# Triangular inverses of two head pairs' chunks: four 64x64 diagonal blocks at a time instead of two 128x128 matrices twice

## The chip, the cores and the metric

The kernel runs on one core of a Trainium2 chip. The metric is the device time of one execution in microseconds; the median of 3 runs is 3688.35 us (3687.65 to 3692.61). PE is TensorE (its matmuls; PEld its weight loads), DVE is VectorE, ACT is ScalarE, POOL is GpSimd.

## The reference

Two model blocks run one after the other on 256 tokens of width 2048 in float32. The change touches two branches of the second block: RWKV-7 (16 heads of 64, in 8 pairs) and the gated delta rule (GDN, 8 heads of 128, in 4 pairs). Both are recurrences over time that the kernel computes in two chunks of 128 tokens. Of the GDN branch the reference says:

```
    lower = jnp.einsum('nbhcd,nbhsd->nbhcs', k_beta, k) * decay_strict
    eye = jnp.eye(GDN_CHUNK, dtype=q.dtype)
    t_mat = lax.linalg.triangular_solve(eye + lower, jnp.broadcast_to(eye, lower.shape),
                                        left_side=True, lower=True)
    u = jnp.einsum('nbhcs,nbhse->nbhce', t_mat, v * beta[..., None])
    w = jnp.einsum('nbhcs,nbhsd->nbhcd', t_mat, k_beta * jnp.exp(g_cum)[..., None])
```

RWKV's step is written in the reference as a scan over single tokens (state times decay, plus two outer products). In chunks it needs the same thing: the inverse of the identity plus a strictly lower triangular 128x128 matrix per head and chunk.

## The kernel before

Weights stream from memory in tiles of 128x1024. ScalarE rounds each to a high part (`whi`, line 276), VectorE forms the rest (`wlo`, line 280), and PE multiplies three times per tile (lines 287 to 289, `mm3`): these are the dense products, with 128x128 weights and 256 or 512 moving columns. They are made by generators in a queue; `fill` runs the next one up to its next tile (24 or 12 products).

The RWKV pairs (`rwkv_pair`) and then the GDN pairs (`gdn_pair`) are generators as well. `weave` keeps up to two pairs going, steps each in turn and, by a credit of 0.44 (RWKV) or 0.6 (GDN) per step, calls `fill` between steps. So a pair's small products stand on PE between runs of dense ones. All engines work off their queues in order; the order is fixed when the program is made, by the order of the code and by a scheduler that may pull ready work ahead.

A pair has two heads and two chunks, so four matrices L to invert. `inverse2` takes two of them (128x128, side by side in a tile of 256 columns) and starts from Y, the inverse of the 2x2 diagonal blocks (lines 1727 to 1733: mask with M1, transpose, subtract from the identity). Five times it doubles the blocks, b = 2, 4, 8, 16, 32: with L masked to the block half it forms Z by a product (line 1738), transposes Y (line 1740), ScalarE takes both out of PSUM (line 1742), a second product (line 1747) gives the correction, and VectorE subtracts it (line 1748). Products are full 128x128 though Y is zero outside its diagonal blocks of up to 64. The closing step fills in the 64x64 block between the two diagonal blocks of 64 (lines 1751 to 1765) with 64x64 products (lines 1754 and 1763) and transposes (line 1759). `both` steps the two calls of `inverse2` of a pair in turn, and a `yield` stands behind each half of a step, where other work may be put. There are 24 calls.

The inverse is used as weights of one 128x128 product per head and chunk: line 1964 in RWKV (64 moving columns), lines 2155, 2156 and 2169 in GDN, where line 2156 has the inverse as the moving side.

Of the kernel before, what the change touches and what calls it, by code (L numbers as in the profile page):

```python
# [11 lines left out]
AF = mybir.ActivationFunctionType  # L12
ALU = mybir.AluOpType
# [69 lines left out]
def layout(i):  # L83
    a = {}
# [31 lines left out]
    p = Pack()  # L116
# [5 lines left out]
    p = Pack()  # L122
# [14 lines left out]
    r = np.arange(128)  # L137
# [19 lines left out]
    G, R, SU = 0, 4112, 8400  # L157
# [18 lines left out]
    for n, nm in enumerate(("s5_c_re_2", "s5_c_im_2")):  # L176
        c = i[nm][0].reshape(32, 2, 16, 64).transpose(1, 3, 0, 2)
# [3 lines left out]
    p = Pack()  # L181
# [17 lines left out]
    p = Pack()  # L199
    lo_ = (r[:, None] > r[None]).astype(np.float32)  # L200
    up = (r[:, None] <= r[None]).astype(np.float32)
    p.add("mask4", np.concatenate([lo_, lo_.T, up, up], 1))
    p.add("M1", (r[:, None] // 2 == r[None] // 2) & (r[:, None] % 2 == 1) & (r[None] % 2 == 0))
    for b in (2, 4, 8, 16, 32):
        p.add(f"M{b}", (r[:, None] // (2 * b) == r[None] // (2 * b)) & (r[:, None] % (2 * b) >= b) & (r[None] % (2 * b) < b))
    e1 = np.zeros((128, 31), np.float32)
    e1[:, 15] = 1
    p.add("E1", e1)
# [24 lines left out]
class K:  # L233
# [1474 lines left out]
        return [x for j in range(8) for x in (self.cm(A["glu"], j, (yh, yl), evg, nk=8), self.cm(A["w2sz"], j, hT, evz, ("sz", j)))]  # L1708


    def inverse2(self, L, res):

        nc = self.nc
        V, PL, mm = nc.vector, nc.gpsimd, nc.tensor.matmul
        cb = lambda n: self.cp(n, "cb")[:, None, :].to_broadcast([128, 2, 128])
        id2 = self.ident[:, None, :].to_broadcast([128, 2, 128])
        v2 = lambda x: x.rearrange("p (a b) -> p a b", a=2)
        T = [slice(128 * i, 128 * i + 128) for i in range(2)]
        U = [slice(256 + 128 * i, 384 + 128 * i) for i in range(2)]

        def masked(b):
            lb = self.r1()
            PL.tensor_tensor(v2(lb), v2(L), cb(f"M{b}"), op=ALU.mult)  # L1723
            return lb


        lm, lb = masked(1), masked(2)
        yield
        ps = self.bank()
        for i in range(2):  # L1730
            nc.tensor.transpose(ps[:, T[i]], lm[:, T[i]], self.ident)
        Y = self.r1()
        V.tensor_tensor(v2(Y), id2, v2(ps[:, 0:256]), op=ALU.subtract)
        yield
        for b in (2, 4, 8, 16, 32):
            ps = self.bank()
            for i in range(2):
                mm(ps[:, T[i]], lb[:, T[i]], Y[:, T[i]], start=True, stop=True)  # L1738
            for i in range(2):
                nc.tensor.transpose(ps[:, U[i]], Y[:, T[i]], self.ident)  # L1740
            zx = self.r2()
            nc.scalar.activation(zx, ps, AF.Copy)
            if b < 32:
                lb = masked(2 * b)
            yield
            for i in range(2):
                mm(ps[:, U[i]], zx[:, U[i]], zx[:, T[i]], start=True, stop=True)  # L1747
            V.tensor_tensor(Y, Y, ps[:, 256:512], op=ALU.subtract)
            yield

        h, l = slice(0, 64), slice(64, 128)
        ps = self.bank()
        for i in range(2):
            mm(ps[h, 64 * i : 64 * i + 64], L[l, 128 * i : 128 * i + 64], Y[l, 128 * i + 64 : 128 * i + 128], start=True, stop=True)  # L1754
        zx = self.r1()
        nc.scalar.activation(zx[h, 0:128], ps[h, 0:128], AF.Copy)
        ps = self.bank()
        for i in range(2):
            nc.tensor.transpose(ps[h, 64 * i : 64 * i + 64], Y[h, 128 * i : 128 * i + 64], self.ident[h, h])
        V.tensor_copy(zx[h, 128:256], ps[h, 0:128])  # L1760
        yield
        for i in range(2):
            mm(ps[h, 128 + 64 * i : 192 + 64 * i], zx[h, 128 + 64 * i : 192 + 64 * i], zx[h, 64 * i : 64 * i + 64], start=True, stop=True)  # L1763
        y = v2(Y)[h, :, 64:128]
        V.tensor_tensor(y, y, ps[h, 128:256].rearrange("p (a b) -> p a b", a=2), op=ALU.subtract)
        yield
        res.append(Y)

    def both(self, a, b):

        for _ in a:
            next(b, None)
            yield
        for _ in b:
            yield


    def rwkv_front(self, pl, hT, kT):
# [86 lines left out]
    def rwkv_pair(self, j, keep, out):  # L1865
        nc, A = self.nc, self.A
        V, ACT, PL, mm = nc.vector, nc.scalar, nc.gpsimd, nc.tensor.matmul
# [12 lines left out]
        lw, a = self.r1(), self.r1()  # L1880
# [47 lines left out]
        ACT.activation(tm, pt, AF.Copy)  # L1928
        yield
        m4 = self.cp("mask4", "cb")  # L1930
        mats, Ls, invs, res = {}, [], [], []
        Ps = [slice(0, 64), slice(64, 128)]
        tks = [slice(0, 128), slice(128, 256)]
        for q in range(2):

            tk = tks[q]
            Ls.append(self.r1())
            pms = [self.bank() for _ in Ps]
            for n, (x, y) in enumerate(((al, be), (ka, al), (be, rh), (ka, rh))):
                for pm, P in zip(pms, Ps):  # L1940
                    mm(pm[:, n * 128 : n * 128 + 128], x[P, tk], y[P, tk], start=True, stop=True)
            for h, pm in enumerate(pms):
                V.tensor_tensor(Ls[q][:, h * 128 : h * 128 + 128], pm[:, 0:128], m4[:, 0:128], op=ALU.mult)  # L1943
                mats[h, q] = self.r2()
                V.tensor_tensor(mats[h, q][:, 0:384], pm[:, 128:512], m4[:, 128:512], op=ALU.mult)
                yield
            res.append([])
            invs.append(self.inverse2(Ls[q], res[q]))
        yield from self.both(*invs)
        py = self.bank()  # L1950
        S1 = None
        for q in range(2):
            U, tk = res[q][0], tks[q]
            v = [tm[:, q * 128 + P.start : q * 128 + P.stop] for P in Ps]
            pa = self.bank()
            if q:
                mm(pa[:, 0:128], al[:, tk], S1, start=True, stop=False)
            for h in range(2):
                mm(pa[:, h * 64 : h * 64 + 64], mats[h, q][:, 0:128], v[h], start=q == 0, stop=q == 0 or h == 1)
            sa = self.r1()  # L1960
            ACT.activation(sa[:, 0:128], pa[:, 0:128], AF.Copy, scale=-1.0)
            yield
            for h in range(2):
                mm(pa[:, 128 + h * 64 : 192 + h * 64], U[:, h * 128 : h * 128 + 128], sa[:, h * 64 : h * 64 + 64], start=True, stop=True)
            V.tensor_copy(sa[:, 128:256], pa[:, 128:256])
# [12 lines left out]
            yield  # L1978
# [3 lines left out]
        sl = [slice(n * 64, n * 64 + 64) for n in range(4)]  # L1982
# [5 lines left out]
        r = self.rstd(self.br, st[:, 2], 4, 64.0, 64e-5)  # L1988
# [7 lines left out]
        f = self.r1()  # L1996
# [99 lines left out]
    def gdn_pair(self, h0, out, T, qk, pss, keep, beta, hb, g, gc, be, kd, gw, rs):  # L2096
        nc, A = self.nc, self.A
        V, ACT, PL, mm = nc.vector, nc.scalar, nc.gpsimd, nc.tensor.matmul
        m4 = self.cp("mask4", "cb")
        low, tri = m4[:, 0:128], m4[:, 256:384]  # L2100
        sets = [(q, d, h0 + d) for q in range(2) for d in range(2)]
        sl = [slice(128 * i, 128 * i + 128) for i in range(4)]
        v4 = lambda x: x.rearrange("p (a b) -> p a b", a=4)
        tk = sl[0:2]
# [8 lines left out]
        E1, E2 = self.r2(), self.r2()  # L2113
        for n, (q, d, h) in enumerate(sets):
            c = gc[:, q, h : h + 1]
# [17 lines left out]
            V.scalar_tensor_tensor(E2[:, sl[n]], pk[:, sl[n]], beta[:, q, h : h + 1], E2[:, sl[n]], op0=ALU.mult, op1=ALU.mult)  # L2133
        V.tensor_tensor(E1, E1, pq, op=ALU.mult)
        yield
        res = [[], []]
        inv = self.both(self.inverse2(E2[:, 0:256], res[0]), self.inverse2(E2[:, 256:512], res[1]))
        next(inv)
        yield

# [8 lines left out]
            next(inv)  # L2149
            yield  # L2150
        yield from inv
        U0, U1 = res[0][0], res[1][0]
        pa, po = self.bank(), self.bank()
        for d in range(2):
            mm(pa[:, sl[d]], U0[:, sl[d]], vt[:, sl[d]], start=True, stop=True)
            mm(pa[:, sl[2 + d]], kt[:, sl[2 + d]], U1[:, sl[d]], start=True, stop=True)
        vn, w, st = self.r2(), self.r1(), self.r1()
        V.tensor_copy(vn[:, 0:256], pa[:, 0:256])
        ACT.activation(w, pa[:, 256:512], AF.Copy, scale=-1.0)
# [6 lines left out]
            mm(po[:, sl[d]], E1[:, sl[d]], vn[:, sl[d]], start=True, stop=True)  # L2166
        yield
        for d in range(2):
            mm(pa[:, sl[2 + d]], U1[:, sl[d]], vt[:, sl[2 + d]], start=True, stop=False)  # L2169
            mm(pa[:, sl[2 + d]], w[:, sl[d]], st[:, sl[d]], start=False, stop=True)  # L2170
        V.tensor_copy(vn[:, 256:512], pa[:, 256:512])
        yield
# [73 lines left out]
```

## Time and profile before

| | us |
|---|---|
| median of 3 runs | 3688.35 |
| profiled execution | 3693.79 |
| its span | 3692.0 |
| PE busy | 3506.5 (95%) |
| VectorE busy | 2494.6 (68%) |
| ScalarE busy | 1626.7 (44%) |
| GpSimd busy | 404.1 (11%) |

RWKV pairs run from 2639 to 3232 us of the span, GDN pairs from 3232 to 3552 us. In the timeline each row is a group of like instructions one behind the other on an engine: when the first started, how long from there to the end of the last, and how many. Matmuls are pipelined, so a row's length counts the way through the array of its last one as well, and rows overlap; the distance between starts is the better measure of what a matmul takes from PE.

### The profile page before, as it was taken

The page shows a single profiled execution, that of the slowest core. Times are in us where ns is not written, and L with a number is a line of the kernel's source. Part 1 is how long each engine was busy: PE and PEld are TensorE (multiplying, and loading weights), DVE is VectorE, ACT ScalarE, POOL GpSimd, SP SyncE. Part 2 cuts the span into 40 slices and gives each one's busy share as a digit, 9 for nine tenths or more (in the row PEclk, how much of TensorE's full clock was granted, in tenths as well). Part 3 has the DMA queues.
Part 4 walks back from the last instruction along what each step waited for, and adds up shares of the span by engine and source line. Part 5 has one row for each costly group of instructions (what it writes and reads, how often), then busy time and mean ns, then how long its engine had stood idle before and what let it go on. Part 6 is the DMA issues. An engine that isn't in the chain of part 4 may idle for free. (4 is left out here: it accounts for less than half of the span.)

```text
span 3692.0 us, 59371 instructions
## 1 busy us (share of the span) xinstructions
PE 3506.5 (95%) x22760; PEld 3124.3 (85%) x22760; DVE 2494.6 (68%) x4329; ACT 1626.7 (44%) x2768; POOL 404.1 (11%) x487
## 2 busy tenths in 40 slices
PE   4799998999999899999999998999999999999998
PEld 4788766999999899988878887786899889888987
DVE  6767787788788654566555557988765556665665
ACT  2245543444444344444545555333444444444444
POOL 0000020000000000000000002333322222021210
PEclk9899998999999999999999999999999999999999
DMA  8875777777544855566666665655533433344455
GB/s 299 279 243 185 230 252 244 256 237 248 175 156 159 266 194 183 183 199 201 211 240 210 209 208 193 200 166 179 169 117 110 144 127 115 115 137 156 147 173 188
DMA packets 237080, 710.83 MB, mean 193 GB/s; under 512 B 33835, under 2 KB 61564, under 8 KB 235516
## 3 DMA queue, kind: packets, MB, share of 16 engines
q1 hardware_dynamic: 196044, 661.59, 54.4%
q10 hardware_dynamic: 40752, 45.44, 3.8%
q8 instruction: 179, 2.93, 0.3%
q14 instruction: 105, 0.86, 0.1%
HBM read 673.86 MB, written 32.55 MB: 191 GB/s over the span
## 5 line engine op out<-in xcount | busy, mean ns | idle before, releaser
L276 ACT ACTIVATE whi<-raw 128x1024 fp32r<-128x1024 f32 (+2 forms) x1006 | 1053.4, 1048 | 1583.5 <-PE acc L288 623.9
L280 DVE TENSOR_TENSOR wlo<-raw,whi 128x1024 fp32r<-128x1024 f32 (+2 forms) x1006 | 1260.6, 1255 | 668.7 <-ACT whi L276 666.9
L287 PE MATMUL acc<-hh,whi 128*128 128x256 f32 x3936 | 1145.3, 291 | 19.1 <-ACT whi L276 16.4
L289 PE MATMUL acc<-hh,wlo 128*128 128x256 f32 x3936 | 1132.0, 288 | 24.4 <-DVE wlo L280 24.0
L288 PE MATMUL acc<-hl,whi 128*128 128x256 f32 x3936 | 1126.5, 286 | 1.0 <-DVE hl L280 1.0
L289 PEld LDWEIGHTS acc<-hh,wlo 128*128 128x128 f32 x3936 | 764.5, 194 | 38.6 <-DVE wlo L280 31.1
L287 PEld LDWEIGHTS acc<-hh,whi 128*128 128x128 f32 x3936 | 765.9, 195 | 32.2 <-ACT whi L276 18.8
L288 PEld LDWEIGHTS acc<-hl,whi 128*128 128x128 f32 x3936 | 764.9, 194 | 2.9 <-DVE hl L280 1.6
L288 PE MATMUL acc<-wlo,wh 128*128 128x512 f32 x1024 | 402.1, 393 | 4.5 <-DVE wlo L280 3.9
L287 PE MATMUL acc<-whi,wh 128*128 128x512 f32 x1024 | 396.2, 391 | 4.8 <-ACT whi L276 3.2
L289 PE MATMUL acc<-whi,wl 128*128 128x512 f32 x1024 | 400.4, 391 | 0.0
L288 PE MATMUL acc<-wlo,hh 128*128 128x512 f32 (+1 forms) x672 | 267.2, 398 | 12.1 <-DVE wlo L280 12.0
L287 PE MATMUL acc<-whi,hh 128*128 128x512 f32 (+1 forms) x672 | 270.8, 406 | 4.6 <-ACT whi L276 3.2
L289 PE MATMUL acc<-whi,hl 128*128 128x512 f32 (+1 forms) x672 | 264.4, 394 | 0.0
L288 PEld LDWEIGHTS acc<-wlo,wh 128*128 128x128 f32 x1024 | 193.5, 189 | 50.9 <-DVE wlo L280 10.5
L287 PEld LDWEIGHTS acc<-whi,wh 128*128 128x128 f32 x1024 | 192.7, 188 | 46.2 <-ACT whi L276 4.5
L289 PEld LDWEIGHTS acc<-whi,wl 128*128 128x128 f32 x1024 | 193.4, 189 | 39.9
L339 DVE SCALAR_TENSOR_TENSOR ada<-raw,u,ada 128x1024 f32<-128x1024 f32 x150 | 194.3, 1295 | 32.9 <-DMA raw<-in_ada_dram 32.0
L288 PEld LDWEIGHTS acc<-wlo,hh 128*128 128x128 f32 x672 | 128.8, 192 | 41.9 <-DVE wlo L280 17.2
L287 PEld LDWEIGHTS acc<-whi,hh 128*128 128x128 f32 x672 | 128.3, 192 | 41.6 <-issue 8.6
L289 PEld LDWEIGHTS acc<-whi,hl 128*128 128x128 f32 x672 | 128.8, 192 | 26.3 <-DVE hl L402 0.2
L1723 POOL TENSOR_TENSOR r<-r,cb 128x256 f32<-128x256 f32 x144 | 132.3, 941 | 155.9 <-DVE r L1943 38.1
(580 smaller groups left out, 4254.0 us busy)
## 6 DMA issues: line engine op xcount, KB each, us to landing
raw<-in_pu_dram SPq DMA_DIRECT2D x256, 512.0 KB, 3.4
raw<-in_pv_dram SPq DMA_DIRECT2D x252, 512.0 KB, 3.5
raw<-in_ada_dram SPq DMA_DIRECT2D x192, 512.0 KB, 4.6
raw<-in_w2gate_dram SPq DMA_DIRECT2D x96, 512.0 KB, 3.4
raw<-in_wo_dram SPq DMA_DIRECT2D x64, 512.0 KB, 4.3
raw<-in_w2br_dram SPq DMA_DIRECT2D x48, 512.0 KB, 3.4
raw<-in_w2g_dram SPq DMA_DIRECT2D x48, 512.0 KB, 3.4
raw<-in_w1e_dram SPq DMA_DIRECT2D x32, 512.0 KB, 4.7
```

The costliest lines, as they stand in the source:

```text
L276: nc.scalar.activation(hi, src, AF.Copy)
L280: self.lo = e.tensor_sub(lo, src, hi.bitcast(F32)).ins
L287: mm(out, shi, mhi, start=start, stop=False)
L288: mm(out, shi, mlo, start=False, stop=False)
L289: mm(out, slo, mhi, start=False, stop=stop)
L339: nc.vector.scalar_tensor_tensor(acc, w, c, acc, op0=ALU.mult, op1=ALU.add)
L1723: PL.tensor_tensor(v2(lb), v2(L), cb(f"M{b}"), op=ALU.mult)
```

## The change

`inverse4` replaces two calls of `inverse2` under `both`. All four matrices of a pair are taken at once, and of each only the two diagonal blocks of 64: GpSimd copies the upper left block of each matrix (partitions 0 to 63) beside the lower right one (partitions 64 to 127), so that one tile of 256 columns holds all eight blocks, four on either half of the partitions. Each product is 64x64; the list `each` goes through the four matrices and for each first through the upper half (rows and columns 0 to 63 of the array), then the lower half (rows and columns 64 to 127). The transposes of the inner steps become products with a 64x64 identity. The masks become 64 columns wide, with a new constant I64. The closing step forms the off-diagonal block and writes it, with the opposite sign, into a second tile R (upper half), beside a copy of the lower diagonal block (lower half). `by_inverse` then applies the inverse in two products: one 64x64 for the first 64 rows of the result, and one with all 128 rows and 64 columns of weights for the other 64. Line 2156 becomes two products in the same manner. The names in the rows below are PE's output and inputs: `sm` is a PSUM bank, `r` a tile of the pair, `cs` the identity, `u` a tile of line 1878's small product, `acc`, `hh`, `hl`, `whi`, `wlo` and `B` belong to the dense products.

The first place is on PE, in the fourth doubling step of the first RWKV pair. Before:

```order
L289 MATMUL acc_25930<-hh_21989,wlo_4412_25934 128x256
L1738 MATMUL sm_25973<-r_4366_25668,r_4404_25892 128x128 x2
L1740 MATMUL sm_25973<-cs_63,r_4366_25668 128x128 x2
L1738 MATMUL sm_25982<-r_4368_25673,r_4407_25901 128x128 x2
L1740 MATMUL sm_25982<-cs_63,r_4368_25673 128x128 x2
L1878 MATMUL sm_25991<-u_3690_22102,r_4423_25992 128x256
```

Now:

```order
L290 MATMUL acc_25942<-hh_21989,wlo_4398_25946 128x256
L1745 MATMUL sm_25988<-r_4363_25670,r_4393_25913 64x64 x8
L1747 MATMUL sm_25988<-cs_63,r_4363_25670 64x64 x8
L1882 MATMUL sm_26009<-u_3690_22102,r_4406_26010 128x256
L1883 MATMUL sm_26009<-u_3690_22102,r_4406_26010 128x256
```

Eight full-size operations in two banks have become sixteen of 64x64 in one bank, at the same place between dense products.

The second place is on PE, the closing step of the same pair. Before:

```order
L289 MATMUL acc_26130<-hh_21989,wlo_26134 128x256
L1754 MATMUL sm_26180<-r_4366_25668,r_4328_25490 64x64 x2
L1759 MATMUL sm_26185<-cs_63,r_4366_25668 64x64 x2
L1754 MATMUL sm_26189<-r_4368_25673,r_4342_25561 64x64 x2
L1759 MATMUL sm_26194<-cs_63,r_4368_25673 64x64 x2
```

Now:

```order
L290 MATMUL acc_26156<-hh_21989,wlo_26160 128x256
L1762 MATMUL sm_26211<-r_4363_25670,r_4328_25490 64x64
L1763 MATMUL sm_26212<-cs_63,r_4363_25670 64x64
L1762 MATMUL sm_26211<-r_4363_25670,r_4328_25490 64x64
L1763 MATMUL sm_26212<-cs_63,r_4363_25670 64x64
```

Product and transpose now alternate one by one (four times; two of the four are shown), not two by two.

The third place is on PE, the first use of the inverse in the same pair. Before:

```order
L1941 MATMUL sm_26283<-r_4451_26107,r_4450_26106 128x128
L1941 MATMUL sm_26284<-r_4451_26107,r_4450_26106 128x128
L1964 MATMUL sm_26259<-r_4481_26262,r_4366_25668 128x64 x2
L287 MATMUL acc_26248<-B_3683_22089,whi_26278 128x256
L288 MATMUL acc_26248<-B_3684_22090,whi_26278 128x256
```

Now:

```order
L1944 MATMUL sm_26308<-r_4432_26133,r_4431_26132 128x128
L1778 MATMUL sm_26284<-r_4460_26287,r_4363_25670 64x64
L1779 MATMUL sm_26284<-r_4460_26287,r_4444_26209 64x64
L1778 MATMUL sm_26284<-r_4460_26287,r_4363_25670 64x64
L1779 MATMUL sm_26284<-r_4460_26287,r_4444_26209 64x64
L288 MATMUL acc_26273<-B_3683_22089,whi_26303 128x256
```

Each of the two products has become two, of different shapes of weights in turn (the sizes in a row are those of the output).

The core of the diff:

```diff
-    for b in (2, 4, 8, 16, 32):
-        p.add(f"M{b}", (r[:, None] // (2 * b) == r[None] // (2 * b)) & (r[:, None] % (2 * b) >= b) & (r[None] % (2 * b) < b))
+    x, y = r[:, None] % 64, np.arange(64)[None]
+    for b in (1, 2, 4, 8, 16, 32):
+        p.add(f"M{b}", (x // (2 * b) == y // (2 * b)) & (x % (2 * b) >= b) & (y % (2 * b) < b))
+    p.add("I64", x == y)
...
-    def inverse2(self, L, res):
+    def inverse4(self, L, res):
...
+        h, l = slice(0, 64), slice(64, 128)
+        PL.tensor_copy(v4(L)[h, :, 64:128], v4(L)[h, :, 0:64])
+        Ld = v4(L)[:, :, 64:128]
+        C = [slice(64 * n, 64 * n + 64) for n in range(4)]
+        G = [slice(256 + 64 * n, 320 + 64 * n) for n in range(4)]
+        each = [(C[n], G[n], P) for n in range(4) for P in (h, l)]
...
         lm, lb = masked(1), masked(2)
         yield
         ps = self.bank()
-        for i in range(2):
-            nc.tensor.transpose(ps[:, T[i]], lm[:, T[i]], self.ident)
+        for c, _, P in each:
+            mm(ps[P, c], lm[P, c], self.ident[P, P], start=True, stop=True)
...
         for b in (2, 4, 8, 16, 32):
             ps = self.bank()
-            for i in range(2):
-                mm(ps[:, T[i]], lb[:, T[i]], Y[:, T[i]], start=True, stop=True)
-            for i in range(2):
-                nc.tensor.transpose(ps[:, U[i]], Y[:, T[i]], self.ident)
+            for c, _, P in each:
+                mm(ps[P, c], lb[P, c], Y[P, c], start=True, stop=True)
+            for c, g, P in each:
+                mm(ps[P, g], Y[P, c], self.ident[P, P], start=True, stop=True)
             zx = self.r2()
-            nc.scalar.activation(zx, ps, AF.Copy)
+            ACT.activation(zx, ps, AF.Copy)
             if b < 32:
                 lb = masked(2 * b)
             yield
-            for i in range(2):
-                mm(ps[:, U[i]], zx[:, U[i]], zx[:, T[i]], start=True, stop=True)
+            for c, g, P in each:
+                mm(ps[P, g], zx[P, g], zx[P, c], start=True, stop=True)
             V.tensor_tensor(Y, Y, ps[:, 256:512], op=ALU.subtract)
             yield
...
+        R = self.r1()
+        PL.tensor_copy(R[l], Y[l])
+        ps, px = self.bank(), self.bank()
+        for n in range(4):
+            mm(ps[h, C[n]], L[l, 128 * n : 128 * n + 64], Y[l, C[n]], start=True, stop=True)
+            nc.tensor.transpose(px[h, C[n]], Y[h, C[n]], self.ident[h, h])
+        zx = self.r2()
+        ACT.activation(zx[h, 0:256], ps[h, 0:256], AF.Copy)
+        V.tensor_copy(zx[h, 256:512], px[h, 0:256])
         yield
...
+        for n in range(4):
+            mm(px[h, G[n]], zx[h, G[n]], zx[h, C[n]], start=True, stop=True)
+        V.tensor_scalar(R[h], px[h, 256:512], -1.0, None, op0=ALU.mult)
         yield
+        res += [Y, R]
+
+    def by_inverse(self, out, U, n, x, stop=True):
+        mm = self.nc.tensor.matmul
+        c = slice(64 * n, 64 * n + 64)
+        mm(out[0:64], U[0][0:64, c], x[0:64], start=True, stop=stop)
+        mm(out[64:128], U[1][:, c], x, start=True, stop=stop)
...
             for h in range(2):
-                mm(pa[:, 128 + h * 64 : 192 + h * 64], U[:, h * 128 : h * 128 + 128], sa[:, h * 64 : h * 64 + 64], start=True, stop=True)
+                self.by_inverse(pa[:, 128 + h * 64 : 192 + h * 64], U, 2 * q + h, sa[:, h * 64 : h * 64 + 64])
...
         for d in range(2):
-            mm(pa[:, sl[d]], U0[:, sl[d]], vt[:, sl[d]], start=True, stop=True)
-            mm(pa[:, sl[2 + d]], kt[:, sl[2 + d]], U1[:, sl[d]], start=True, stop=True)
+            self.by_inverse(pa[:, sl[d]], U, d, vt[:, sl[d]])
+            c, o = slice(128 + 64 * d, 192 + 64 * d), 256 + 128 * d
+            mm(pa[:, o : o + 64], kt[0:64, sl[2 + d]], U[0][0:64, c], start=True, stop=True)
+            mm(pa[:, o + 64 : o + 128], kt[:, sl[2 + d]], U[1][:, c], start=True, stop=True)
...
         for d in range(2):
-            mm(pa[:, sl[2 + d]], U1[:, sl[d]], vt[:, sl[2 + d]], start=True, stop=False)
+            self.by_inverse(pa[:, sl[2 + d]], U, 2 + d, vt[:, sl[2 + d]], stop=False)
```

## Rows read from the trace of the kernel before

**Rows 1.** The page: span, busy time of each engine, granted clock in slices.
```profile
span 3692.0 us, 59371 instructions
...
PE 3506.5 (95%) x22760; PEld 3124.3 (85%) x22760; DVE 2494.6 (68%) x4329; ACT 1626.7 (44%) x2768; POOL 404.1 (11%) x487
...
PEclk9899998999999999999999999999999999999999
```
**Rows 2.** Windows, RWKV and GDN pairs: busy us (instructions), granted clock, DMA.
```profile
core 0: us, PE busy (x) PEld busy (x) DVE busy (x) ACT busy (x) POOL busy (x), PEclk, DMA share, GB/s
2639.00:3232.00 593.00, 580.08 (x4534) 536.37 (x4534) 364.01 (x653) 260.05 (x546) 149.46 (x214) 0.99 0.38 123
3232.00:3552.00 320.00, 314.62 (x2017) 275.21 (x2016) 184.23 (x295) 141.02 (x263) 78.37 (x87) 0.99 0.44 142
```
**Rows 3.** Groups by line: count, busy us, mean ns of one, idle before.
```profile
L1723 POOL TENSOR_TENSOR r<-r,cb 128x256 f32<-128x256 f32 x144 | 132.3, 941 | 155.9 <-DVE r L1943 38.1 <-DVE r L2056 32.4 <-PE sm L1941 15.0
L1738 PE MATMUL sm<-r,r 128*128 128x128 f32 x480 | 74.5, 278 | 0.9 <-DVE r L1748 0.7
L1742 ACT ACTIVATE r<-sm 128x512 f32<-128x512 f32 x120 | 66.8, 594 | 16.2 <-PE sm L1740 15.2
...
L1748 DVE TENSOR_TENSOR r<-r,sm 128x256 f32<-128x256 f32 x120 | 49.7, 419 | 76.4 <-PE sm L1747 52.3 <-issue 8.1 <-ACT whi L276 6.4
L1740 PE MATMUL sm<-cs,r 128*128 128x128 f32 x240 | 45.8, 273 | 0.0
```
**Rows 4.** Timeline, PE, a full-size burst: start us, us to the last end.
```profile
2666.98 0.28 PE L289 MATMUL acc<-hh,wlo 128*128 128x256 f32 x1
2667.10 1.05 PE L1747 MATMUL sm<-r 128*128 128x128 f32 x8
...
2668.11 0.28 PE L288 MATMUL acc<-hl,whi 128*128 128x256 f32 x1
```
**Rows 5.** Timeline, PE, a use of the inverse.
```profile
2842.80 0.55 PE L1964 MATMUL sm<-r,r 128*128 128x64 f32 x4
```
**Rows 6.** Timeline, PE, a 64x64 burst on one corner.
```profile
2772.86 0.28 PE L289 MATMUL acc<-hh,wlo 128*128 128x256 f32 x1
2773.07 0.67 PE L1763 MATMUL sm<-r 64*64 64x64 f32 x8
2773.68 0.39 PE L287 MATMUL acc<-hh,whi 128*128 128x256 f32 x1
2773.90 0.28 PE L288 MATMUL acc<-hl,whi 128*128 128x256 f32 x1
```
**Rows 7.** Timeline, PE, the closing step's products and transposes.
```profile
2767.31 0.28 PE L289 MATMUL acc<-hh,wlo 128*128 128x256 f32 x1
2767.52 0.44 PE L1754 MATMUL sm<-r,r 64*64 64x64 f32 x4
2767.89 0.30 PE L1759 MATMUL sm<-cs,r 64*64 64x64 f32 x2
2768.12 0.44 PE L1754 MATMUL sm<-r,r 64*64 64x64 f32 x4
2768.50 0.30 PE L1759 MATMUL sm<-cs,r 64*64 64x64 f32 x2
2768.72 0.39 PE L287 MATMUL acc<-hh,whi 128*128 128x256 f32 x1
2768.95 0.28 PE L288 MATMUL acc<-hl,whi 128*128 128x256 f32 x1
```
**Rows 8.** Timeline, PE, 64-row products on upper and lower rows.
```profile
2652.33 0.28 PE L289 MATMUL acc<-hh,wlo 128*128 128x256 f32 x1
2652.54 1.16 PE L1941 MATMUL sm<-r,r 64*128 64x128 f32 x16
...
2653.85 0.28 PE L288 MATMUL acc<-hl,whi 128*128 128x256 f32 x1
```
**Rows 9.** Timeline, PE, products on four column strips.
```profile
2363.19 1.07 PE L1637 MATMUL sm<-r,r 128*32 128x256 f32 x16
```

More of the change, by code (lines that the diff above doesn't have):

```diff
@@ L202, in layout @@
     p.add("mask4", np.concatenate([lo_, lo_.T, up, up], 1))
-    p.add("M1", (r[:, None] // 2 == r[None] // 2) & (r[:, None] % 2 == 1) & (r[None] % 2 == 0))
-    for b in (2, 4, 8, 16, 32):
-        p.add(f"M{b}", (r[:, None] // (2 * b) == r[None] // (2 * b)) & (r[:, None] % (2 * b) >= b) & (r[None] % (2 * b) < b))
+    x, y = r[:, None] % 64, np.arange(64)[None]
+    for b in (1, 2, 4, 8, 16, 32):
+        p.add(f"M{b}", (x // (2 * b) == y // (2 * b)) & (x % (2 * b) >= b) & (y % (2 * b) < b))
+    p.add("I64", x == y)
     e1 = np.zeros((128, 31), np.float32)
@@ L1708, in s5_back @@
         return [x for j in range(8) for x in (self.cm(A["glu"], j, (yh, yl), evg, nk=8), self.cm(A["w2sz"], j, hT, evz, ("sz", j)))]
-    def inverse2(self, L, res):
+    def inverse4(self, L, res):
         nc = self.nc
[L1714 to L1719, printed above, removed]
+        V, ACT, PL, mm = nc.vector, nc.scalar, nc.gpsimd, nc.tensor.matmul
+        v4 = lambda x: x.rearrange("p (a b) -> p a b", a=4)
+        cb = lambda n: self.cp(n, "cb")[:, None, :].to_broadcast([128, 4, 64])
+        h, l = slice(0, 64), slice(64, 128)
[4 more added lines that the diff above has]
+        each = [(C[n], G[n], P) for n in range(4) for P in (h, l)]
         def masked(b):
             lb = self.r1()
-            PL.tensor_tensor(v2(lb), v2(L), cb(f"M{b}"), op=ALU.mult)
+            PL.tensor_tensor(v4(lb), Ld, cb(f"M{b}"), op=ALU.mult)
             return lb
@@ L1729, in inverse2 @@
         ps = self.bank()
-        for i in range(2):
-            nc.tensor.transpose(ps[:, T[i]], lm[:, T[i]], self.ident)
+        for c, _, P in each:
+            mm(ps[P, c], lm[P, c], self.ident[P, P], start=True, stop=True)
         Y = self.r1()
-        V.tensor_tensor(v2(Y), id2, v2(ps[:, 0:256]), op=ALU.subtract)
+        V.tensor_tensor(v4(Y), cb("I64"), v4(ps[:, 0:256]), op=ALU.subtract)
         yield
@@ L1745, in inverse2 @@
             yield
-            for i in range(2):
-                mm(ps[:, U[i]], zx[:, U[i]], zx[:, T[i]], start=True, stop=True)
+            for c, g, P in each:
+                mm(ps[P, g], zx[P, g], zx[P, c], start=True, stop=True)
             V.tensor_tensor(Y, Y, ps[:, 256:512], op=ALU.subtract)
             yield
[L1751 to L1760, printed above, removed]
+        R = self.r1()
[7 more added lines that the diff above has]
+        V.tensor_copy(zx[h, 256:512], px[h, 0:256])
         yield
[L1762 to L1765, printed above, removed]
+        for n in range(4):
+            mm(px[h, G[n]], zx[h, G[n]], zx[h, C[n]], start=True, stop=True)
+        V.tensor_scalar(R[h], px[h, 256:512], -1.0, None, op0=ALU.mult)
         yield
[L1767 to L1775, printed above, removed]
+        res += [Y, R]
[4 more added lines that the diff above has]
+        mm(out[64:128], U[1][:, c], x, start=True, stop=stop)
     def rwkv_front(self, pl, hT, kT):
@@ L1930, in rwkv_pair @@
         m4 = self.cp("mask4", "cb")
-        mats, Ls, invs, res = {}, [], [], []
+        mats, L, U = {}, self.r2(), []
         Ps = [slice(0, 64), slice(64, 128)]
@@ L1936, in rwkv_pair @@
             tk = tks[q]
-            Ls.append(self.r1())
             pms = [self.bank() for _ in Ps]
@@ L1942, in rwkv_pair @@
             for h, pm in enumerate(pms):
-                V.tensor_tensor(Ls[q][:, h * 128 : h * 128 + 128], pm[:, 0:128], m4[:, 0:128], op=ALU.mult)
+                n = 256 * q + 128 * h
+                V.tensor_tensor(L[:, n : n + 128], pm[:, 0:128], m4[:, 0:128], op=ALU.mult)
                 mats[h, q] = self.r2()
@@ L1946, in rwkv_pair @@
                 yield
-            res.append([])
-            invs.append(self.inverse2(Ls[q], res[q]))
-        yield from self.both(*invs)
+        yield from self.inverse4(L, U)
         py = self.bank()
@@ L1952, in rwkv_pair @@
         for q in range(2):
-            U, tk = res[q][0], tks[q]
+            tk = tks[q]
             v = [tm[:, q * 128 + P.start : q * 128 + P.stop] for P in Ps]
@@ L2135, in gdn_pair @@
         yield
-        res = [[], []]
-        inv = self.both(self.inverse2(E2[:, 0:256], res[0]), self.inverse2(E2[:, 256:512], res[1]))
+        U = []
+        inv = self.inverse4(E2, U)
         next(inv)
@@ L2151, in gdn_pair @@
         yield from inv
-        U0, U1 = res[0][0], res[1][0]
         pa, po = self.bank(), self.bank()
         for d in range(2):
-            mm(pa[:, sl[d]], U0[:, sl[d]], vt[:, sl[d]], start=True, stop=True)
-            mm(pa[:, sl[2 + d]], kt[:, sl[2 + d]], U1[:, sl[d]], start=True, stop=True)
+            self.by_inverse(pa[:, sl[d]], U, d, vt[:, sl[d]])
+            c, o = slice(128 + 64 * d, 192 + 64 * d), 256 + 128 * d
+            mm(pa[:, o : o + 64], kt[0:64, sl[2 + d]], U[0][0:64, c], start=True, stop=True)
+            mm(pa[:, o + 64 : o + 128], kt[:, sl[2 + d]], U[1][:, c], start=True, stop=True)
         vn, w, st = self.r2(), self.r1(), self.r1()
```

## The prediction

> **What bounds the kernel now.** I read first the busy shares and slices of the page: TensorE (PE) is busy 95% of a 3692.0 us span, at 0.8 or more of its full clock in every slice [rows 1]. Then the busy times of the two stretches that hold all the edited code: the eight RWKV head pairs (2639 to 3232 us) and the four GDN pairs (3232 to 3552 us). There PE is busy 580.08 of 593 us and 314.62 of 320 us, at a granted clock of 0.99, while VectorE has work for 364 and 184 us, ScalarE for 260 and 141 us, GpSimd for 149 and 78 us [rows 2]. So PE bounds both stretches, and its idle time in them is only 13 + 5 = 18 us. The steps of an inverse lie between runs of the dense products (lines 287 to 289), usually 12 or 24 at a time, and these need nothing from the inverse. A microsecond of PE's queue is therefore a microsecond of the kernel; one on the other three engines is not. They lose work all the same: of the 120 evictions of 594 ns on ScalarE, the 120 subtractions of 419 ns on VectorE and the 144 masks of 941 ns on GpSimd half go, some 36, 25 and 68 us [rows 3]; 24 half-width copies and 12 final subtractions change places on GpSimd and VectorE. I value all of that at nothing, because PE hides it; at most it can give back part of the 18 us.
>
> A busy PE row says little of what a small product costs, since products overlap. I price from starts: from the last dense start ahead of a burst to the second dense start behind it, less two dense spacings of 0.12 us.
>
> - Full-array products: the burst of eight 128x128 passes costs 2668.11 - 2666.98 - 0.24 = 0.89 us, 0.111 a pass, and nothing for entering or leaving [rows 4]. A float32 product is two passes (line 1738 has 240 products and 480 rows), a transpose one (line 1740: 240) [rows 3]. With 64 moving columns a pass still takes 0.11 us: four of line 1964 last 0.55 us with a last one of some 0.22 [rows 5].
> - 64x64 products on one corner: the burst of eight passes costs 2773.90 - 2772.86 - 0.24 = 0.80 us. Eight passes start (0.67 - 0.22) / 7 = 0.064 us apart with the first gap the longest; I use 0.0585, half of 0.111 plus a little for the half-width weights, 0.47 us together. The other 0.33 us is the price of going into the small shape and back: the first pass starts 0.21 us behind the dense one, and behind the burst two dense starts lie 0.22 us apart, not 0.12 [rows 6].
> - A change between two small shapes: line 1754 (product) and line 1759 (transpose, also 64x64) in turn cost 2768.95 - 2767.31 - 0.24 = 1.40 us for 12 passes. Less 0.70 for passes and 0.33 for in and out, 0.37 us is left for three changes inside: 0.12 each [rows 7].
> - Two parts of the array at once: line 1941 sends 64-row products to the upper and the lower rows in turn. Sixteen passes with 128 columns last 1.16 us, so they start (1.16 - 0.27) / 15 = 0.059 us apart, half of 0.111: two go at once. In and out cost 2653.85 - 2652.33 - 0.24 - 0.89 = 0.39 us [rows 8].
>
> **The change part by part.**
>
> *Passes.* Before, 24 calls of the inverse: 960 product passes (480 + 480) and 288 transposes (240, and 2 first ones a call) at 0.1105 are 138 us; the closing step's 10 passes a call at 0.0585 are 14 us; the uses of the inverse, 64 passes in RWKV and 48 in GDN, at 0.111, are 12 us. Together 164 us. After, 12 calls: 8 products first and 5 x 24 later, two passes each since the transposes become products with the identity, are 256 passes a call, 3072 in all. No row shows 64x64 products on opposite corners. Bounds: 0.0585 a pass if they go one by one [rows 6], half of it, 0.0293, if two go at once as in [rows 8]. I take 0.0293, since in [rows 8] too it is the alternation by rows that pairs them: 90 us. The closing step has the same 20 passes per four blocks: 14 us. The uses double: 128 passes at 0.0585 in RWKV and 96 at 0.111 in GDN (128 moving columns or 128-column weights): 18 us. Together 122 us. Saved on passes: 42 us.
>
> *Changes of shape.* In the order of instructions I counted how often neighbours on PE differ in tile shape from the first RWKV pair to the end: 200 before, 608 after, 408 more. The causes can be seen in the three places shown: every one of the 11 bursts of an inverse ahead of its closing step is now 64x64 between dense 128x128 work, where it was 128x128; the closing step alternates product and transpose one by one; and each use becomes a 64x64 product followed by one with all 128 rows and 64 columns. Of the 408, 131 are between two small shapes (168 against 37), the rest are in or out. At 0.12 and at 0.33 / 2 = 0.165 us that is 16 + 46 = 62 us. Bounds: all at 0.12 is 49 us, all at 0.39 / 2 = 0.195 is 80 us. The shape of 128 rows by 64 columns is in no row; if going between it and 64x64 cost nothing, some 70 changes fall out and 62 becomes 53.
>
> The Trainium skill, "TensorEngine Tiling (Array Packing)", section Tiling Modes, says that changing the tiling mode, not just the tile, drains the engine. It speaks against this change, agrees with [rows 6] and [rows 7], and by it the 128x64 shape pays like the others (62), not 53.
>
> *Waits.* Ahead of each burst stand mostly the same 12 or 24 dense products, and ScalarE now has one eviction to do, not two in a row, so I add no wait. Where the order leaves few dense products between steps (the first GDN inverse and the last), the second half of a pair used to fill the gap of the first; now the burst is shorter and PE waits for the eviction. The chain is shorter by one eviction and one subtraction as well, so I put that at zero, with 3 us either way. GpSimd's new copy of the four diagonal blocks stands ahead of the first masks, but the first product waits for two operations there, where the second inverse used to wait for three. The copy of the lower half has the closing step's two bursts to land in. The constants lose 320 columns in one load early on: nothing.
>
> **Sum.** 62 - 42 = 20 us more. Against the profiled execution's own 3693.79 us (span 3692.0 and 1.8 around it) that is 3714. The median of the runs shown is 3688.35, 5 us lower, so I forecast 3708 us. From the bounds: 49 - 42 - 3 = 4 to 80 - 42 + 3 = 41 us more, 3692 to 3729.
>
> **The rivals.**
>
> *The corners do not overlap.* Then the 3072 passes cost 0.0585 each, 90 us more: 3798 us. For it: both corners write into one PSUM bank (sm_25988 in the order), whereas line 1941 writes its two row halves into two banks. Against it: line 1637 of the S5 part puts four column strips into one bank, and sixteen passes of 256 columns take 1.07 us, under a third of what 16 x 0.22 would be [rows 9]; and the two corners write different partitions. The same page of the Trainium skill, section Restrictions and Gotchas, says that different row tiles cannot access one PSUM bank at the same time; taken to the letter it gives this rival. No row here has two row tiles in one bank.
>
> *The chain, not PE's queue, ends the waits (faster).* The place is the inverse's step with little dense work behind it. One eviction and one subtraction fewer is 0.59 + 0.42, about 1.0 us per step, 60 us over 60 steps. If PE's idle time in both stretches comes from that, up to 18 us returns; with changes of shape at the lowest price (7 us net) the time is 3688 + 7 - 18 = 3677 us. It decides from the point where more idle time returns than the net price of PE's queue, 7 to 20 us. Against it: 18 us is all the idle time there is, and dense products stand in most of these gaps.
>
> *The gain on passes and the changes cancel.* If bursts of the other pair's work touch the small bursts more often than the order suggests and the unseen shape is free, 49 - 9 - 42 = -2 to some +7 us: 3686 to 3695 us, no change that can be told.
>
> **How the numbers follow.** Forecast 68% (3695 to 3729), corners one by one 9%, cancelled 14%, faster 9%. What a measurement of this kernel can tell from no change is about 0.2%, 7 us. Slower by more: 68 + 9 = 77%; within: 14%; faster: 9%. For the range I keep the forecast and most of the cancelled case and leave out the serial corners and the faster case: 3686 to 3730.
>
> **What would show it.** In the profile after: the products of the inner steps start about 0.03 us apart on average (a burst of 32 passes lasts about 1.1 us); if it lasts near 2 us the corners are serial. Behind each small burst the second dense start lies 0.22 us away; PE's instruction count rises by some 1900 and its idle time in both stretches stays under 25 us. Of the 408 changes 249 fall to the RWKV pairs and 159 to the GDN pairs; at 62 / 408 = 0.15 each, less 32 and 10 us for the passes, the RWKV stretch grows by some 6 us and the GDN stretch by some 14; nothing ahead of 2630 us moves. I am wrong if the dense starts behind a 64x64 burst are not delayed, if the uses of the inverse cost no changes, or if PE's idle time falls to near zero.

## The result, and the profile after

The changed kernel takes 3721.72 us (median of 7, 3703.63 to 3728.63) against 3692.61 us (7) for the kernel before in the same session: ratio 1.0078, 95% interval 1.0059 to 1.0097. Two later sets of 6 gave 1.0072 and 1.0073. So it is 29 us slower here and 26 to 27 us in the two later sets; 20 were forecast.

The page of the changed kernel answers to [rows 1]: 1936 more matmuls, less work on the other three engines, PE busy for 95% of the span as before.

```profile
span 3720.2 us, 62859 instructions
...
PE 3529.3 (95%) x24696; PEld 3098.8 (83%) x24696; DVE 2449.1 (66%) x4233; ACT 1597.5 (43%) x2696; POOL 344.2 (9%) x439
```

The windows of the two stretches, cut at the first RWKV product, the first GDN product and the first product of the tail: first two rows of before (a finer cut of [rows 2]), then two of after.

```profile
2639.15:3232.93 593.78, 580.82 (x4539) 537.02 (x4539) 364.74 (x654) 260.02 (x546) 149.46 (x214) 0.99 0.38 123
3232.93:3557.66 324.73, 319.42 (x2033) 279.00 (x2034) 188.83 (x301) 143.78 (x266) 78.37 (x87) 0.99 0.44 142
```
```profile
2641.13:3240.48 599.35, 582.55 (x5844) 518.28 (x5844) 340.15 (x592) 242.35 (x499) 108.64 (x182) 1.00 0.41 124
3240.48:3589.54 349.06, 344.40 (x2680) 280.13 (x2681) 171.41 (x268) 134.19 (x241) 59.07 (x71) 0.95 0.43 131
```

RWKV is 5.6 us longer (6 forecast), GDN 24.3 (14 forecast), at a clock of 0.95 instead of 0.99. PE is idle for 17 us in RWKV (13 before) and 5 us in GDN (5 before). Some dense work has changed stretch: 25 dense products (3.0 us) stand in RWKV now and stood in GDN before, and the tail behind is 3.7 us shorter by 16 that GDN took over.

PE's timeline in the changed kernel, the two bursts of an inner step (they answer to [rows 4]):

```profile
2664.89 0.28 PE L290 MATMUL acc<-hh,wlo 128*128 128x256 f32 x1
2665.10 0.68 PE L1745 MATMUL sm<-r,r 64*64 64x64 f32 x16
2665.61 0.63 PE L1747 MATMUL sm<-cs,r 64*64 64x64 f32 x16
2666.18 0.38 PE L288 MATMUL acc<-hh,whi 128*128 128x256 f32 x1
2666.40 0.28 PE L289 MATMUL acc<-hl,whi 128*128 128x256 f32 x1
...
2669.03 0.28 PE L290 MATMUL acc<-hh,wlo 128*128 128x256 f32 x1
2669.24 0.68 PE L1754 MATMUL sm<-r 64*64 64x64 f32 x16
2669.85 0.39 PE L288 MATMUL acc<-hh,whi 128*128 128x256 f32 x1
2670.07 0.28 PE L289 MATMUL acc<-hl,whi 128*128 128x256 f32 x1
```

From the dense start ahead to the second one behind, less 0.24: 32 passes cost 1.27 us, 16 cost 0.80. At 0.0293 a pass plus 0.33 for in and out the forecast's prices give 1.27 and 0.80.

The closing step (answers to [rows 7]; product and transpose stand four times in turn, and five of the eight rows are left out) and a use in RWKV (answers to [rows 5]):

```profile
3298.92 0.39 PE L290 MATMUL acc<-whi,hl 128*128 128x512 f32 x1
3299.24 0.33 PE L1762 MATMUL sm<-r,r 64*64 64x64 f32 x2
3299.49 0.24 PE L1763 MATMUL sm<-cs,r 64*64 64x64 f32 x1
3299.66 0.32 PE L1762 MATMUL sm<-r,r 64*64 64x64 f32 x2
...
3300.95 0.50 PE L288 MATMUL acc<-whi,hh 128*128 128x512 f32 x1
3301.28 0.39 PE L289 MATMUL acc<-wlo,hh 128*128 128x512 f32 x1
```
```profile
2848.61 0.28 PE L290 MATMUL acc<-hh,wlo 128*128 128x256 f32 x1
2848.82 0.33 PE L1778 MATMUL sm<-r,r 64*64 64x64 f32 x2
2849.07 0.33 PE L1779 MATMUL sm<-r,r 128*64 128x64 f32 x2
2849.33 0.32 PE L1778 MATMUL sm<-r,r 64*64 64x64 f32 x2
2849.59 0.33 PE L1779 MATMUL sm<-r,r 128*64 128x64 f32 x2
2849.85 0.39 PE L288 MATMUL acc<-hh,whi 128*128 128x256 f32 x1
2850.07 0.28 PE L289 MATMUL acc<-hl,whi 128*128 128x256 f32 x1
```

Twelve passes of the closing step cost 1.91 us (two dense steps of 0.227 us taken off, as these have 512 columns), the use 1.22 us where it was 0.44. The two places of use in GDN cost 2.95 and 2.30 us where they were 0.89 each.

What the forecast has no term for is the opening of the first GDN pair: the two longest waits of PE in these stretches, and the granted clock in the windows around them (the last two rows are the 30 us from 2 us ahead of the first GDN product, before and after).

```profile
PE acc L288 <- DVE r L2053: 3.4, 1, 3.4
PE sm L2110 <- DVE rsy L2093: 2.7, 1, 2.7
```
```profile
3240.00:3254.00 14.00, 10.18 (x36) 8.07 (x36) 5.22 (x16) 2.72 (x8) 2.34 (x4) 0.62 0.13 40
3254.00:3260.00 6.00, 5.90 (x14) 4.64 (x15) 4.37 (x11) 0.69 (x2) 4.63 (x7) 0.50 0.00 0
...
3230.93:3260.93 30.00, 26.26 (x160) 21.67 (x159) 23.64 (x42) 12.32 (x26) 15.51 (x17) 1.00 0.35 110
3238.48:3268.48 30.00, 24.56 (x151) 18.95 (x152) 17.09 (x37) 8.29 (x21) 8.85 (x12) 0.72 0.16 50
```

L2093 ends VectorE's chain of reciprocal square roots, some 8 us behind PE's last L2071. In the order 46 dense products (5.5 us) now lie over it; before there were 69 (8.2 us). PE waits 2.7 us, which fall to the end of the RWKV stretch, and its granted clock falls to the lower level (0.50, 1.2 GHz): the pair's first 128x128 passes start 0.21 us apart, not 0.11. Behind the pair's first transposes (L2148) stand 15 dense products, where 43 stood before. The first of them waits for VectorE to empty its accumulator (`acc`), and VectorE comes to that only behind the pair's own work:

```profile
3253.57 0.48 DVE L2053 TENSOR_SCALAR r<-acc,cp 128x256 f32<-128x256 f32 x1
3254.10 0.79 PE L288 MATMUL acc<-whi,hh 128*128 128x512 f32 x1 [3.44 <-DVE r L2053]
```

Before, PE was at its 43 dense products meanwhile, and its longest wait there was 1.2 us.

### The profile page after: what moved, and what is told of

The parts are those of the page before. It is cut to its first block, busy times and chain, and to the rows that moved or that the text cites. A ratio compares the mean times of both kernels' runs of the same rounds, so it can differ in the third digit from the quotient of the medians.

```text
span 3720.2 us, 62859 instructions
## 1 busy us (share of the span) xinstructions
PE 3529.3 (95%) x24696; PEld 3098.8 (83%) x24696; DVE 2449.1 (66%) x4233; ACT 1597.5 (43%) x2696; POOL 344.2 (9%) x439
## 5 line engine op out<-in xcount | busy, mean ns | idle before, releaser
L1162 DVE TENSOR_SCALAR oh<-u,pickT 128x128 f32<-128x128 f32 x256 | 72.3, 282 | 44.4 <-PE sm L1164 44.4
```

The source lines that it names most:

```text
L1162: V.tensor_scalar(a, iota, pT[:, 0, t : t + 1], None, op0=ALU.is_equal)
```

## The experiments

The theory: the loss comes from small tile shapes on PE's queue, those of the uses above all, and the opening of GDN adds to it. The rivals: the number of passes makes the loss, not the shapes; the corners do not overlap; the opening is worth nothing.

| run | edit | median us (runs) | ratio to before, 95% |
|---|---|---|---|
| e1, e9 | the changed kernel again | 3713.44 (6), 3712.89 (6) | 1.0072 (1.0054 to 1.0090), 1.0073 (1.0051 to 1.0095) |
| e2, e10 | two dense steps ahead of GDN | 3714.23 (6), 3710.85 (6) | 1.0078 (1.0058 to 1.0097), 1.0069 (1.0042 to 1.0095) |
| e3 | e5 and e6 together | 3675.67 (12) | 0.9971 (0.9959 to 0.9982) |
| e4 | e3 and e2 | 3671.59 (11) | 0.9954 (0.9940 to 0.9968) |
| e5 | inverse in one full tile, uses whole again | 3689.86 (12) | 1.0002 (0.9987 to 1.0017) |
| e6 | closing transposes made products | 3697.02 (12) | 1.0019 (1.0002 to 1.0037) |
| e7 | before, uses split | 3716.81 (6) | 1.0068 (1.0042 to 1.0094) |
| e8 | upper corner first, then lower | 3752.51 (4) | 1.0173 (1.0143 to 1.0202) |
| e11 | before, fewer dense products at the opening | 3691.55 (12) | 1.0015 (1.0001 to 1.0029) |
| e12 | e4, credit 0.40 | 3666.32 (7) | 0.9951 (0.9932 to 0.9969) |

**The uses (e5, e7).** The inverse is written into one 128x128 tile per matrix (a memset and two copies on GpSimd, and VectorE's last step), and a use is one product again. Of the edit, the lines of the use:

```diff
-        c = slice(64 * n, 64 * n + 64)
-        mm(out[0:64], U[0][0:64, c], x[0:64], start=True, stop=stop)
-        mm(out[64:128], U[1][:, c], x, start=True, stop=stop)
+        mm(out, U[0][:, 128 * n : 128 * n + 128], x, start=True, stop=stop)
```

> The full 128x128 tile for the uses alone; the closing step still alternates products and transposes. My theory (each use pays for two shape changes): the 16 places of use in RWKV fall by 0.77 us (12 us), the eight in GDN by 2.06 and 1.41 us (14 us): 26 us below the changed kernel, ratio to the kernel before 1.000 (0.998 to 1.002). Rival D (it is the doubled passes, not the shapes): 64 + 48 passes less at 0.06 to 0.11 us, at most 9 us below the changed kernel, ratio 1.005. Rival C (the copies that build the tile make the uses wait): ratio above 1.003, with waits for GpSimd ahead of the uses.

Ratio 1.0002: the loss is gone, as expected, though the two waits of the opening are still in e5's profile. A use in its timeline, 2837.15 - 2836.47 - 0.24 = 0.44 us:

```profile
2836.47 0.28 PE L290 MATMUL acc<-hh,wlo 128*128 128x256 f32 x1
2836.59 0.55 PE L1779 MATMUL sm<-r,r 128*128 128x64 f32 x4
2836.95 0.36 PE L288 MATMUL acc<-hh,whi 128*128 128x256 f32 x1
2837.15 0.28 PE L289 MATMUL acc<-hl,whi 128*128 128x256 f32 x1
```

e7 goes the other way: the kernel before, its old inverse kept, with its uses split as in the changed kernel:

> The kernel before, with the uses of its inverse alone split as in the changed kernel: a 64x64 product and one of 128 rows by 64 columns for each 128x128 product, the inverse itself as before. My theory: the 26 us of the uses come back alone, ratio to the kernel before 1.007 (1.005 to 1.009), nearly the whole of the changed kernel's loss, since the inverse itself saves about as much in passes as it pays in shapes. Rival E (the loss lies in the inverse's inner steps): 0 to 9 us, ratio below 1.0025.

Ratio 1.0068, 25 us. Split uses alone cost nearly what the whole change costs, and the new inverse with whole uses costs nothing that can be told from zero: shown from both sides. The GDN stretch of e7, with the clock at 0.99:

```profile
3246.86:3585.64 338.78, 333.63 (x2081) 286.26 (x2082) 188.40 (x301) 143.51 (x266) 77.30 (x87) 0.99 0.41 137
```

It is 14.1 us longer than the stretch before, what the two places of use are worth (4 pairs at 2.06 and 1.41 us, 14 us).

**The closing step (e6, e3).** The transposes become products with the identity:

```diff
-            nc.tensor.transpose(px[h, C[n]], Y[h, C[n]], self.ident[h, h])
+            mm(px[h, C[n]], Y[h, C[n]], self.ident[h, h], start=True, stop=True)
```

> The closing step's four transposes become products with the identity, nothing else. My theory: the 12 bursts of four products and four transposes fall from 1.90 to 0.80 us, as those of 16 passes in one shape do: 13 us below the changed kernel, ratio to the kernel before 1.0040 (1.002 to 1.006). Rival D (changing between product and transpose costs nothing in a 64x64 tile; the burst is long since its two row halves write two banks one after the other): the burst stays above 1.7 us, the ratio at 1.007.

In e6's timeline the same burst, of 16 passes now (of its eight pairs of rows, six are left out):

```profile
3284.10 0.39 PE L290 MATMUL acc<-whi,hl 128*128 128x512 f32 x1
3284.42 0.27 PE L1762 MATMUL sm<-r,r 64*64 64x64 f32 x1
3284.43 0.27 PE L1763 MATMUL sm<-cs,r 64*64 64x64 f32 x1
...
3284.88 0.22 PE L1762 MATMUL sm<-r,r 64*64 64x64 f32 x1
3284.89 0.22 PE L1763 MATMUL sm<-cs,r 64*64 64x64 f32 x1
3285.03 0.50 PE L288 MATMUL acc<-whi,hh 128*128 128x512 f32 x1
3285.37 0.39 PE L289 MATMUL acc<-wlo,hh 128*128 128x512 f32 x1
```

It costs 3285.37 - 3284.10 - 0.455 = 0.82 us, 1.1 less with four passes more; twelve times that is 13 us. The ratio fell from 1.0072 (e1) to 1.0019, 20 us, just past the range expected; the difference to 13 is within the intervals. Only these four operations of the burst changed, and it still writes two banks, so rival D is out.

> Two parts of the new inverse undone. The closing step writes the inverse into one full 128x128 tile (one memset and two copies on GpSimd, one half on VectorE), so each use is a single 128x128 product as before; and the closing step's four transposes become products with the identity, so that it no longer alternates between product and transpose. My theory (shape changes are the price): the 16 uses in RWKV fall from 1.21 to about 0.44 us (12 us), the two places of use in each of 4 GDN pairs from 2.95 and 2.30 to 0.89 each (14 us), the 12 closing bursts from 1.90 to about 0.80 us (13 us): 39 us below the changed kernel, 8 to 12 us below the kernel before, and the opening still waits. Rival C (the copies that build the full tile make the use wait, so the gain is lost to waits on GpSimd): less than 20 us below the changed kernel. Rival D (the passes, not the shapes, cost: corners one by one): the closing step gains 0 to 4 us, the uses 4 us at most.

Both edits: 38 us below e1 and 12 below the kernel before, as expected. Taking these changes out turns the loss into a gain. Beside e5 alone the closing products are worth 11 us, beside e6 alone the full tile 18; the two edits' shares are no closer known than 11 to 20 and 18 to 26 us.

**The turns (e8).**

```diff
-        each = [(C[n], G[n], P) for n in range(4) for P in (h, l)]
+        each = [(C[n], G[n], P) for P in (h, l) for n in range(4)]
```

> The changed kernel with the four products on the upper corner first and the four on the lower behind them, instead of in turn. My theory: the pairs overlap because neighbours in the queue sit on opposite corners, and a product of two passes on one corner follows the next one at 0.0585 us a pass; without turns the 256 passes of a call cost up to 0.029 us more each, 3072 x 0.029 = 90 us, and a 32-pass burst takes about 2.0 instead of 1.27 us: ratio to the kernel before 1.020 to 1.032. Rival F (the corners never overlapped, the small passes are just short, or the queue looks far enough ahead to pair them in any order): the ratio stays at 1.007.

The mechanism came out, the size did not: 37 us more, not 90. The burst in e8:

```profile
2659.35 0.28 PE L290 MATMUL acc<-hh,wlo 128*128 128x256 f32 x1
2659.56 0.96 PE L1754 MATMUL sm<-r 64*64 64x64 f32 x16
2660.45 0.39 PE L288 MATMUL acc<-hh,whi 128*128 128x256 f32 x1
2660.67 0.28 PE L289 MATMUL acc<-hl,whi 128*128 128x256 f32 x1
```

It costs 1.08 instead of 0.80 us, and the 32-pass burst 1.66 instead of 1.27; six bursts of the one and five of the other in each of 12 calls would make some 43 us. By the spacing of the starts in e8's records, the lower corner's first pass starts just behind the fifth of the upper corner's eight, so some of them still overlap: PE does not start these strictly in the order of its queue.

**The opening (e1, e2, e4, e9 to e12).** e1 and e9 repeat the changed kernel.

> The changed kernel once more, as the base for the others beside it. My theory: two parts. PE's queue (62 us of shape changes against 42 us of passes saved) gives about +20 us; the other 8 to 10 us come at the opening of the first GDN pair, where only 46 dense products (5.5 us) stand between the last L2071 and the first L2110, against 69 (8.2 us) before, while VectorE's chain of square roots between them takes some 8 us: PE waits 2.7 and 3.4 us and its granted clock lies at half for about 15 us. So 3703 to 3729 us, median near 3718, 26 us or more above the kernel before, and the runs with the lower mean clock are the longer ones. Rival A (queue alone): the opening is an accident of one execution and the median lies near 3708 to 3712.

> The changed kernel again, as the base for the next one and for a third profile of the opening of the first GDN pair. Two profiles showed 2.7 us of waiting there and a granted clock at half for 13 to 15 us. If that belongs to the order: again 2.7 us ahead of the first L2110, a mean clock of 0.85 or less in the 30 us from 2 us ahead of it (0.72 and 0.77 so far), ratio 1.0060 to 1.0085.

Both times the same two waits, a clock of 0.77 in the 30 us around them, and GDN stretches of 350.7 and 347.7 us: the opening belongs to the order, not to one execution. The time alone does not tell, as e1's 3713 us lie between theory and rival. The edit of e2 and e10, ahead of GDN's weave:

```diff
+        self.fill(2)
```

> Two dense steps are put ahead of the first GDN pair: 65 dense products, not 46, now stand between the last L2071 and the first products of the pair. Nothing else changes. My theory: PE's wait ahead of the pair's first product falls from 2.7 to below 1 us, the granted clock stays near 1.0 there, and the time falls by 6 to 10 us against the changed kernel, to about 20 us above the kernel before. Rival A (the opening costs nothing, since PE's dense work is only moved): within 3 us of the changed kernel. Rival B (the wait moves: the dense products taken here are missing behind the transposes L2148, and ScalarE and VectorE still hold the banks): the first wait goes, a second of 3 us or more stays, and at most 4 us are won.

> The changed kernel with two dense steps ahead of the first GDN pair, again. The first time the profile had a GDN stretch 10 us shorter, the times were the same (3714.2 against 3713.4 us). My theory that the opening costs the time: 5 us or more below the changed kernel, ratio at most 1.006. Rival A (what the clock does not lose here it loses elsewhere, so the opening is worth 0 to 3 us): ratio within 0.001 of the changed kernel's, and the profile shows dips of the clock in stretches where PE is busy throughout.

The longest waits of PE in e10 from 3205 to 3262 us: the first of the two is gone, the second stays.

```profile
PE acc L288 <- DVE r L2053: 3.4, 1, 3.4
PE sm L2071 <- ACT r L2067: 0.3, 2, 0.2
```

The times stay the same (26 and 27 us above before on the means), though both profiles have GDN stretches 9 to 11 us shorter, 4 of them moved dense work. Rival B, at most 4 us, holds for this edit, and so does e10's rival A; my 6 to 10 us do not.

> The full tile, the closing products and the two dense steps ahead of the first GDN pair together (64 dense products there). If the parts add: 39 + 6 to 10 us below the changed kernel, 3668 to 3678 us, 14 to 24 us below the kernel before. Rival (the two overlap in the GDN stretch, or the opening's wait only moves): the same as without the two dense steps.

e4 is 4 us below e3: a small gain, and their intervals overlap. e11 takes dense work from the old kernel's opening (`0.44` to `0.48` in RWKV's weave, which moves the same 25 dense products into RWKV as the change does):

> The other way round: the kernel before, with its RWKV pairs taking dense steps at a credit of 0.48 instead of 0.44, so that only 22 dense products (not 69) are left between the last L2069 and the first L2108. The inverse is the old one. My theory that the opening costs time: PE waits some 5 us there and the clock falls, 6 to 12 us above the kernel before, ratio 1.0015 to 1.0035. Rival A: the wait is there in the profile, the ratio is 0.999 to 1.001.

```profile
PE sm L2108 <- DVE rsy L2091: 4.5, 1, 4.5
PE acc L287 <- DVE r L2051: 3.4, 1, 3.4
```

With both waits and a clock of 0.77 there, 0.15% (0.01 to 0.29): some 5 us, where I expected 6 to 12. Last, e4 with `0.40` for `0.44` in RWKV's weave:

> The full tile, the closing products, two dense steps ahead of the first GDN pair, and a credit of 0.40 instead of 0.44 for the dense steps between the RWKV pairs' work: 76 dense products stand ahead of the first GDN products and 30 behind its first transposes (64 and 18 with a credit of 0.44, 46 and 15 in the changed kernel, 69 and 43 in the kernel before). If both waits of the opening cost time, the second (3.4 us for VectorE's L2053) shrinks too, the clock there stays above 0.9, and the time falls 2 to 6 us below the 0.9954 of the kernel with a credit of 0.44, to a ratio of 0.9938 to 0.9949. Rival: the wait comes back elsewhere, since the dense work held back in the RWKV pairs leaves their own steps with less cover: ratio 0.9950 or above, with more idle time of PE in the RWKV stretch.

In e12's waits L2053 is down to 0.7 us and L2093 gone; the windows show the clock at 1.00 for the 30 us around the opening and 0.99 over GDN. It is the fastest, 18 us (0.5%) below the kernel before, but not to be told from e4: the ratio is the rival's, not mine, though PE's idle time in RWKV is the same (12.0 us against 11.6 in e4), so the rival's wait did not come either. Together these comparisons (e2, e10, e4, e11, e12) put the opening between 0 and some 10 us; more closely it is not settled.

## Why the prediction was right, and where it was not

- **The bound** was right: PE is idle for 17 and 5 us in the two stretches, and the time went with PE's queue. Less work on the other engines brought nothing that shows.
- **Passes** were right: 0.0293 us on alternating corners. The rival of corners one by one is out: e8 shows what is lost without turns. The Trainium skill, "TensorEngine Tiling (Array Packing)", section Restrictions and Gotchas, says that different row tiles cannot access one PSUM bank at the same time. Here two corners that write disjoint partitions of one bank (L1754) cost 0.80 us for 16 passes, and two row halves that write two banks as much (0.82, e6), so for disjoint partitions the measurement decides against it.
- **Changes of shape** were right in price. By the forecast's prices a use in RWKV comes to 1.16 us, the closing step to 1.87, the first place of use in GDN to 2.95; 1.22, 1.91 and 2.95 were measured. The Trainium skill, "TensorEngine Tiling (Array Packing)", section Tiling Modes, says that changing the tiling mode, not just the tile, drains the engine. The use agrees: 1.22 us with products of 64x64 and 128x64 in turn, 0.44 in one shape (e5). At these prices the uses cost 12 us in RWKV and 14 in GDN, so the forecast's 20 us are 26 for the uses less 6 saved in the inverse itself, a split it did not draw. e7 shows 25 for the uses; e5, which keeps the 6 and the opening, comes out even, which fits the 6 but does not fix them. The changes in [rows 7] and in the closing step are between products and transposes of one size, 64x64; that sentence of the Trainium skill does not speak of them, and e6 prices them.
- **The RWKV stretch** met its 6 us by luck: 3.0 of the 5.6 are dense products that stood in GDN before, and 2.7 are the first wait.
- **Waits and clock** failed: "so I add no wait". I looked at the dense products ahead of the bursts of the inverse, not at how many the new order leaves over VectorE's chain ahead of the first GDN pair, and I priced all of PE's work at the clock of 0.99. Two waits of 6.1 us stand there now. In the GDN stretch as a whole PE is idle no longer than before (4.7 against 5.3 us), so its surplus, 24 us against the 14 of the forecast, goes with the lower clock, 0.95. e7, with the split uses at 0.99, has the 14; e5, with the new inverse and whole uses at 0.96, is 9 us longer than before. In time the surplus is not settled: e11 puts such an opening at some 5 us, which with the 20 makes 25 of the measured 26 to 29 (an estimate), but e2 and e10 won nothing.
- **The total** of 3721.72 us is 14 above the forecast of 3708: 9 of them in the change, and 4 because the kernel before ran at 3692.61 us beside it, not at 3688.35.
- **Nothing ahead of 2630 us moves**: the program there is the same, yet the RWKV pairs began at 2632.8, 2634.0 and 2641.1 us in three profiles of one kernel. One profile cannot tell 8 us there.

## What to carry to other kernels

Count the places where a small tile shape stands alone between full-size work: each costs about 0.33 us here, and 0.12 to 0.16 for each change within, which a use of two products pays in full. Go compact inside a chain that stays in one shape, and give the result back at full size. After any edit, count again what the order leaves over the long chains of other engines, also where nothing was edited.

## What the runs showed of the hardware that was not expected

- Two 64x64 passes start about 0.01 us apart, and the next two some 0.05 later. This holds on opposite corners that write one bank (L1754) and on the two row halves over the same columns that write two (L1762 and L1763 in e6). On one corner each pass starts 0.0585 behind the last [rows 6].
- A product and a transpose in turn cost nothing between them at 128x128 in the kernel before (12 passes 1.32 us, 0.11 each), but do at 64x64 (e6).
- The granted clock also falls where PE never idles. A window of e1:

```profile
3380.00:3400.00 20.00, 20.00 (x102) 14.95 (x101) 9.53 (x19) 6.03 (x8) 3.32 (x4) 0.88 0.49 148
```

In the profiles of the changed kernel (after, e1, e9), every fall of the clock in GDN behind the opening comes in or right behind a run of small products: L2110 (16 rows), L2114 and L1769 (64x64), or a closing step with a use and L1769. In e10 three of these runs pass without a fall, so what decides it is open. It may be why mending one wait in e2 and e10 shortened the GDN stretch in the profiles and not the time.
